# VectorE in GpSimd's place after the last attention head, values ahead of the out block, and final roots for groups of rows

## The chip, the cores and the metric

The kernel runs on one core of a Trainium2 chip. A core has TensorE (PE, matrix products into PSUM banks), VectorE (DVE), ScalarE (ACT), GpSimd (POOL) and SyncE (SP, which here only issues DMAs), each with its own queue of instructions in order. They wait for each other through semaphores. The metric is the device time of one execution in microseconds; less is better.

## What is computed

One layer of a hybrid step: an attention head group and an mLSTM head group side by side, an output projection over both, a SwiGLU feed-forward part, and a last RMS norm. There are 128 context tokens and 1024 latent tokens, so nine rows of 128 tokens (row 0 is context), and a width of 1024. Cut to what the change touches:

```python
mix = jnp.concatenate([attn_o, hm], axis=-1) @ w_out
x = x + g1 * mix
h2 = rmsnorm(x, norm2_w) * (1 + sc2) + sh2
g, u = jnp.split(h2 @ w_gu, 2, axis=-1)
x = x + g2 * ((jax.nn.silu(g) * u) @ w_down)
y = x * lax.rsqrt(jnp.mean(x * x, axis=-1, keepdims=True) + EPS) * final_norm_w
```

Products are made more exact by splitting operands into a high and a low part, so that a product is three matmuls: high by high, high by low, low by high.

## The kernel before, in words

**Attention.** `step(n)` is called for the 64 pairs of a row and a head, and then for some more n until all tasks are done. Its order is written out by hand: products of scores, then `fl.run("PE")`, then the value products of a finished pair of heads (`value_products`, L1054: 18 matmuls of the transposed weights phT and plT with the values into `po`), then the softmax of this head. `fl` is a filler: tasks such as the output projection of a row (`mix_task`) yield the engine that they need next and a cost, and `fl.run` resumes those that fit.

**Output projection and second norm.** `value_sums` scales the value products on ACT (L1059, L1060, `ol`) and adds two halves on POOL into `oT` (L1062). When a row's four pairs are in, `mix_copies` casts `oT` to a high part on ACT (L1420) and subtracts it on POOL for the low part (L136, `kst`, by L1421). `out_block` (L1143 to L1145) makes 12 matmuls into a bank, for each half of the width. `add_gated` multiplies by the gate on DVE (L1134) and adds to the row on POOL (L1137). Then comes the norm: squares on ACT (L1426, `jk`), a root of small instructions on DVE (L1190 to L1197, `r`), the scaled row on ACT (L1433, `y`), transposes on PE (L115), scale and shift half on ACT (L1452) and half on DVE (L1454, `fl`), and the split into high and low parts `h`: casts on ACT (L1462), subtractions on POOL (L136, by L1463). Two out blocks are made for a row. The last row, 8, has no attention step behind it.

**Feed-forward part.** It begins behind row 8's out blocks and the transposes of row 7's norm; row 8's norm is made within it. Its first gate products (L1181 to L1183) use rows whose `h` has long been ready. Weights are loaded (`braw`, `wdt`), measured, scaled and split (`wpair`, L1606 on ACT and L1607 on DVE). DVE and POOL add slices of `h` up (`sk`, L1724 on DVE, L1726 on POOL). From here on a list scheduler sets the order within each engine's queue. The PSUM pool gives out eight banks; `bank()` takes the next.

**End.** After the last group's gates, the final loop goes over the nine rows. For each half of a row, PE makes 12 down products (L1834 to L1836) into a bank; DVE scales by the gate (L1136) and adds to the row (L1137); ACT sums the squares (L1921). After a row's first half POOL multiplies it by the norm's gain `fw` (L1924). After the second half DVE makes the root (L1923, then the twelve instructions of `rsqrt`, L126 to L132, ten of them each waiting for the one before). ACT scales the first half (L1927) and DVE the second, with `fw` in the same instruction (L1928). Each half leaves as a DMA of 256 KB (L1929 from ACT's queue, L1930 from SP's).

Of the kernel before, what the change touches and what calls it, by code (L numbers as in the profile page):

```python
# [8 lines left out]
F32 = mybir.dt.float32  # L9
# [10 lines left out]
P = 128  # L20
# [26 lines left out]
def hybrid_step(ctx: ExitStack, tc: tile.TileContext, I: dict, O: dict):  # L47
# [1009 lines left out]
    def value_sums(b, j, po):  # L1057
# [3 lines left out]
        for g in range(2):  # L1061
            pool.tensor_tensor(out=oT[b][64 * g : 64 * g + 64, j, :], in0=ol[:, 1, g * P : (g + 1) * P],  # L1062
                               in1=ol[:, 0, g * P : (g + 1) * P], op=ALU.add)
# [204 lines left out]

    fl = Filler(PE=3.5, ACT=1.9, DVE=2.0)
# [116 lines left out]
    def mix_task(b):  # L1386
        yield "ACT", 0.5, 1, 0, lambda: b in done and (b == 0 and "pools" in at or since(("atO", b - 1, 1)))
        mix_copies(b)
        for n in range(2):
# [4 lines left out]
            add_gated(x1[b], ps, gx[n] if b == 0 else gs[n], n, pool)  # L1394
# [23 lines left out]
    def mix_copies(b):  # L1418
        th, tl = mix
        nc.scalar.copy(th, oT[b])  # L1420
        sub(tl, oT[b], th.bitcast(F32), "pool")  # L1421
# [35 lines left out]
    def norm_split(b, both):  # L1457
        c, i = divmod(b, CB)
        for half in range(2):
# [3 lines left out]
            sub(ol, full, oh, "pool")  # L1463
# [27 lines left out]
    def step(n):  # L1491
# [5 lines left out]
        fl.run("PE")  # L1497
# [3 lines left out]
        elif n % 2 == 1 and (n - 3) // 2 in pairs:  # L1501
            m = (n - 3) // 2
            two = pairs.pop(m)
            now = [value_products(heads[2 * m][0], m % 4, NB, m % 4 // 2, lambda t, i: two[t][:, :, i, :])]
        if n < len(heads):
# [154 lines left out]
    psum["mm"] = ctx.enter_context(tc.tile_pool(name="p8", bufs=8, space=PSUM, reuse_waits="tile"))  # L1660
    pieces[1].load()
# [250 lines left out]
    for b in range(NB):  # L1912
        st = fp.tile([P, 4], F32, name=nm("st"), tag="fst", bufs=4)
        for n in range(2):
            ps = bank()
            for j in range(0, g["nf"], 2):
                down_products(ps, g, j, b, ws[n][j // 2])
            add_gated(x1[b], ps, gate2(b, n), n, inv=g["inv"])
            v = x1[b][:, n * 512 : (n + 1) * 512]
            jk = ft.tile([P, D], BF16, name=nm("jk"), tag="t2", bufs=3)  # L1920
            act(jk[:, 0:512], v, AF.Square, accum_out=st[:, n : n + 1])  # L1921
            if n == 0:
                dve.tensor_scalar(out=st[:, 2:3], in0=st[:, 0:1], scalar1=1.0 / D, scalar2=EPS, op0=ALU.mult, op1=ALU.add)  # L1923
                pool.tensor_tensor(out=v, in0=v, in1=fw[:, 0:512], op=ALU.mult)  # L1924
        r = rsqrt(fp, st[:, 1:2], 1, 1.0 / D, CB, st[:, 2:3])
        lo, hi = x1[b][:, 0:512], x1[b][:, 512:1024]
        act(lo, lo, AF.Copy, scale=r)  # L1927
        dve.scalar_tensor_tensor(out=hi, in0=hi, scalar=r, in1=fw[:, 512:1024], op0=ALU.mult, op1=ALU.mult)  # L1928
        nc.scalar.dma_start(yrow(b)[:, 0:512], lo)  # L1929
        dma(yrow(b)[:, 512:1024], hi)  # L1930
# [52 lines left out]
```

## Time and profile before

| | |
|---|---|
| median of 3 runs | 1612.08 us (1606.82 to 1614.46) |
| the profiled execution's own time | 1611.04 us |
| its span | 1609.3 us |
| mean granted clock of PE | 0.954 |
| PE busy | 1456.1 us, 90% of the span |
| DVE busy | 1141.5 us, 71% |
| ACT busy | 790.6 us, 49% |
| POOL busy | 265.9 us, 17% |

Times in the profile are microseconds from the start of the span. A row of an engine's timeline gives start, length, engine, line and operation, and in brackets the idle time ahead of it with the instruction that ended it. The stages are: input projections and the mLSTM part until about 440, attention heads until about 812, the output projection and norm of the last row until about 866, the feed-forward part until 1590.9 (PE's last product), and the last roots and stores until 1609.3.

### The profile page before, as it was taken

The page shows a single profiled execution, that of the slowest core. Times are in us where ns is not written, and L with a number is a line of the kernel's source. Part 1 is how long each engine was busy: PE and PEld are TensorE (multiplying, and loading weights), DVE is VectorE, ACT ScalarE, POOL GpSimd, SP SyncE. Part 2 cuts the span into 40 slices and gives each one's busy share as a digit, 9 for nine tenths or more (in the row PEclk, how much of TensorE's full clock was granted, in tenths as well). Part 3 has the DMA queues.
Part 4 walks back from the last instruction along what each step waited for, and adds up shares of the span by engine and source line. Part 5 has one row for each costly group of instructions (what it writes and reads, how often), then busy time and mean ns, then how long its engine had stood idle before and what let it go on. Part 6 is the DMA issues. An engine that isn't in the chain of part 4 may idle for free. (4 is left out here: it accounts for less than half of the span.)

```text
span 1609.3 us, 23125 instructions
## 1 busy us (share of the span) xinstructions
PE 1456.1 (90%) x8417; PEld 900.6 (56%) x8417; DVE 1141.5 (71%) x2572; ACT 790.6 (49%) x1504; POOL 265.9 (17%) x284
## 2 busy tenths in 40 slices
PE   5899999899596799987769999999999999999995
PEld 2655666576354577765545556546545645656542
DVE  3944355848866687876758898777767867787478
ACT  3744343435465666777756535425504523654123
POOL 0411021403216522333344000000000000000001
PEclk8899999999788899998879999999999999999998
DMA  9445452301175689656544323432433332322303
GB/s 350 128 134 154 104 142 66 72 6 19 34 174 108 119 188 204 130 96 122 89 121 135 115 92 118 131 92 93 133 115 99 112 120 90 118 92 81 104 1 118
DMA packets 281687, 181.83 MB, mean 113 GB/s; under 512 B 167302, under 2 KB 253782, under 8 KB 281574
## 3 DMA queue, kind: packets, MB, share of 16 engines
q1 hardware_dynamic: 280150, 177.96, 42.3%
q10 hardware_dynamic: 1424, 2.40, 0.4%
q8 instruction: 66, 1.08, 0.3%
q14 instruction: 47, 0.39, 0.1%
HBM read 122.71 MB, written 19.29 MB: 88 GB/s over the span
## 5 line engine op out<-in xcount | busy, mean ns | idle before, releaser
L1606 ACT ACTIVATE wpair<-braw,fv 128x1024 f16<-128x1024 f32 x84 | 93.7, 1139 | 171.7 <-PE mm L1836 94.9
L1835 PE MATMUL mm<-wd,hl 128*128 128x512 f16 x396 | 149.8, 379 | 0.0
L1834 PE MATMUL mm<-wd,hl 128*128 128x512 f16 x396 | 149.6, 379 | 0.0
L1836 PE MATMUL mm<-wd,hl 128*128 128x512 f16 x396 | 142.3, 379 | 0.0
L1111 PE MATMUL S<-kst,qT 128*128 128x512 f32 (+1 forms) x384 | 98.4, 397 | 47.2 <-ACT pr L1119 45.4
L1181 PE MATMUL mm<-h,wpair 128*128 128x384 f16 x416 | 137.3, 330 | 4.3 <-DVE r L1190 3.2
L1183 PE MATMUL mm<-h,wpair 128*128 128x384 f16 x416 | 136.8, 330 | 2.4 <-DVE wpair L1607 2.4
L1182 PE MATMUL mm<-h,wpair 128*128 128x384 f16 x416 | 137.2, 330 | 0.0
L1607 DVE SCALAR_TENSOR_TENSOR wpair<-braw,fv,wpair 128x1024 f16<-128x1024 f32 x84 | 106.5, 1281 | 37.4 <-ACT wpair L1606 37.4
L1924 POOL TENSOR_TENSOR x<-x,fw 128x512 f32<-128x512 f32 x9 | 11.7, 1304 | 710.8 <-ACT jk L1921 710.8
L500 PE MATMUL wi<-ipair,hT 128*128 128x384 f16 (+2 forms) x384 | 124.4, 325 | 2.8 <-ACT ipair L217 2.8
L501 PE MATMUL wi<-ipair,hT 128*128 128x384 f16 (+2 forms) x384 | 124.5, 324 | 0.0
L502 PE MATMUL wi<-ipair,hT 128*128 128x384 f16 (+2 forms) x384 | 123.9, 323 | 0.0
L1115 DVE TENSOR_REDUCE st<-S 128x1 f32<-128x1152 f32 x64 | 86.7, 1355 | 44.8 <-PE S L1111 44.2
L1518 DVE SCALAR_TENSOR_TENSOR pl<-pr,st,ph 128x1152 f16<-128x1152 f32 x64 | 94.3, 1474 | 28.2 <-ACT ph L1510 25.6
L1510 ACT ACTIVATE ph<-pr,st 128x1152 f16<-128x1152 f32 x64 | 80.3, 1254 | 68.8 <-issue 59.7
L1111 PEld LDWEIGHTS S<-kst,qT 128*128 128x128 f32 x384 | 70.9, 210 | 71.7 <-ACT pr L1119 57.8
L1119 ACT ACTIVATE pr<-S,st 128x1152 f32<-128x1152 f32 x64 | 78.0, 1219 | 28.3 <-DVE st L1115 27.7
L1136 DVE SCALAR_TENSOR_TENSOR t<-mm,gm,gl 128x512 f32<-128x512 f32 x96 | 70.6, 744 | 29.0 <-PE mm L1836 28.8
L1137 DVE TENSOR_TENSOR x<-x,t 128x512 f32<-128x512 f32 x108 | 78.1, 736 | 1.3
L1737 PE MATMUL mm<-h,wpair 128*128 128x384 f16 x240 | 78.2, 326 | 0.0
L1736 PE MATMUL mm<-h,wpair 128*128 128x384 f16 x240 | 78.2, 326 | 0.0
(462 smaller groups left out, 3625.7 us busy)
## 6 DMA issues: line engine op xcount, KB each, us to landing
wd<-wd_d SPq DMA_DIRECT2D x58, 512.0 KB
braw<-in_w_gu_dram SPq DMA_DIRECT2D x44, 512.0 KB
a4s<-in_w_ada_dram SPq DMA_DIRECT2D x32, 512.0 KB
wdt<-in_w_down_dram SPq DMA_DIRECT2D x22, 512.0 KB
wd_d<-wdt SPq DMA_DIRECT2D x22, 512.0 KB
aw<-in_w_ada_dram SPq DMA_DIRECT2D x16, 512.0 KB
x<-in_x_sample_dram SPq DMA_DIRECT2D x16, 512.0 KB
iraw<-in_w_in_dram SPq DMA_DIRECT2D x32, 256.0 KB
```

What stands on the lines that cost most here:

```text
L500: mm(ps[:, :n], ah, wh[:, k % 2, c0 : c0 + n], start=(k == 0), stop=False)
L501: mm(ps[:, :n], ah, wl[:, k % 2, c0 : c0 + n], start=False, stop=False)
L502: mm(ps[:, :n], al, wh[:, k % 2, c0 : c0 + n], start=False, stop=(k == KD - 1))
L1111: mm(S[:, lo:hi], qTs[b][:, h, :], kst[kv][:, t, lo:hi], start=(t == 0), stop=(t == 1))
L1181: mm(ps, wh[:, k, :], th[:, k, :], start=(k == 0), stop=False)
L1182: mm(ps, wh[:, k, :], tl[:, k, :], start=False, stop=False)
L1183: mm(ps, wl[:, k, :], th[:, k, :], start=False, stop=(k == KD - 1))
L1518: dve.scalar_tensor_tensor(out=pl, in0=pr, scalar=st[:, 3:4], in1=ph, op0=ALU.mult, op1=ALU.subtract)
L1607: dve.scalar_tensor_tensor(out=t[:, 1], in0=raw, scalar=sc, in1=t[:, 0], op0=ALU.mult, op1=ALU.subtract)
L1834: mm(ps, ah, w[:, k, 0], start=(j + k == 0), stop=False)
L1835: mm(ps, ah, w[:, k, 1], start=False, stop=False)
L1836: mm(ps, al, w[:, k, 0], start=False, stop=(j + k == g["nf"] - 1))
```

## The change

There are four parts.

First, `side()` names the engine for additions and subtractions in the tasks: DVE from the first step without a head (n of 64 and more), POOL before. It is used in `value_sums`, in the second instruction of `add_gated` in `mix_task`, in `mix_copies` and in the norm's split.

Second, in steps with n of 64 and more the value products and their sums stand ahead of `fl.run("PE")`.

Third, ahead of the feed-forward part `bank()` is called twice, and the two tiles are not used.

Fourth, the final loop goes over groups of rows (0, 1, 2), (3, 4, 5), (6, 7) and (8). A group has one root for all of its rows (L1938 adds the two sums of squares, then `rsqrt` over 3, 2 or 1 columns). POOL multiplies both halves of a row by `fw` (L1937) except the last half of row 8. ACT scales whole rows (L1943), and a whole row leaves as one DMA of 512 KB, in turn from ACT's and SP's queue (L1944). Row 8 is finished as before (L1947, L1948).

```diff
@@ value_sums
-            pool.tensor_tensor(out=oT[b][64 * g : 64 * g + 64, j, :], in0=ol[:, 1, g * P : (g + 1) * P],
+            side().tensor_tensor(out=oT[b][64 * g : 64 * g + 64, j, :], in0=ol[:, 1, g * P : (g + 1) * P],
...
+    def side():
+        return dve if fl.step >= len(heads) else pool
...
@@ mix_task
-            add_gated(x1[b], ps, gx[n] if b == 0 else gs[n], n, pool)
+            add_gated(x1[b], ps, gx[n] if b == 0 else gs[n], n, side())
@@ mix_copies
-        sub(tl, oT[b], th.bitcast(F32), "pool")
+        sub(tl, oT[b], th.bitcast(F32), "pool" if side() is pool else "dve")
@@ norm_split
-            sub(ol, full, oh, "pool")
+            sub(ol, full, oh, "pool" if side() is pool else "dve")
@@ step(n)
-        fl.run("PE")
+        if n < len(heads):
+            fl.run("PE")
...
+        if n >= len(heads):
+            for v in late + now:
+                value_sums(*v)
+            late[:], now = [], []
+            fl.run("PE")
...
     psum["mm"] = ctx.enter_context(tc.tile_pool(name="p8", bufs=8, space=PSUM, reuse_waits="tile"))
+    for _ in range(2):
+        bank()
...
-    for b in range(NB):
-        st = fp.tile([P, 4], F32, name=nm("st"), tag="fst", bufs=4)
...
-            act(jk[:, 0:512], v, AF.Square, accum_out=st[:, n : n + 1])
-            if n == 0:
-                dve.tensor_scalar(out=st[:, 2:3], in0=st[:, 0:1], scalar1=1.0 / D, scalar2=EPS, op0=ALU.mult, op1=ALU.add)
-                pool.tensor_tensor(out=v, in0=v, in1=fw[:, 0:512], op=ALU.mult)
-        r = rsqrt(fp, st[:, 1:2], 1, 1.0 / D, CB, st[:, 2:3])
...
+    for rows in ((0, 1, 2), (3, 4, 5), (6, 7), (8,)):
+        st = fp.tile([P, 2, CB], F32, name=nm("st"), tag="fst", bufs=2)
+        ss = fp.tile([P, CB], F32, name=nm("ss"), tag="fss", bufs=2)
+        k = len(rows)
...
+                act(jk[:, 0:512], v, AF.Square, accum_out=st[:, n, i : i + 1])
+                if n == 0 or k > 1:
+                    pool.tensor_tensor(out=v, in0=v, in1=fw[:, n * 512 : (n + 1) * 512], op=ALU.mult)
+        dve.tensor_tensor(out=ss[:, 0:k], in0=st[:, 0, 0:k], in1=st[:, 1, 0:k], op=ALU.add)
+        r = rsqrt(fp, ss[:, 0:k], k, 1.0 / D, CB)
+        for i, b in enumerate(rows):
+            ri = r[:, i : i + 1]
+            if k > 1:
+                act(x1[b], x1[b], AF.Copy, scale=ri)
+                (dma if i % 2 else nc.scalar.dma_start)(yrow(b), x1[b])
+                continue
...
```

The rows below are the instructions as each built program holds them for an engine, in order; a bracket names the engines and queues that a row waits for.

TensorE behind the transposes for row 6's norm, before: the end of row 7's second out block (`mm_8132`), and then the last pair of value products, which is row 8's (`phT_8024`, `plT_8025`). Row 8's two out blocks follow these.

```order
L1144 MATMUL mm_8132<-whi_6782,kst_4270 128x512
L1145 MATMUL mm_8132<-whi_6781,kst_4271 128x512
L1054 LDWEIGHTS vs [waits DMAHW6_49,DMAHW4_49]
L1054 MATMUL po_4797<-phT_8024,vs 128x256 [waits Activation_49]
L1054 LDWEIGHTS vs [waits DMAHW7_49]
L1054 MATMUL po_4797<-plT_8025,vs 128x256 [waits DMAHW5_49]
```

The same place in the changed kernel: the pair stands right behind the transposes (L115).

```order
L115 MATMUL mm_8114<-ident,y_8093 128x128 [waits DVE_49]
L115 MATMUL mm_8114<-ident,y_8093 128x128 x3
L1054 LDWEIGHTS vs [waits DMAHW6_49,DMAHW4_49]
L1054 MATMUL po_4797<-phT_8024,vs 128x256 [waits Activation_49]
L1054 LDWEIGHTS vs [waits DMAHW7_49]
L1054 MATMUL po_4797<-plT_8025,vs 128x256 [waits DMAHW5_49]
```

Row 7's out block (12 matmuls, now `mm_8155`) follows behind the pair's 18, and then row 8's two.

POOL's queue in the same stretch, before: sums of values, subtractions, additions to the row, and then the first sums `sk`.

```order
L1062 TENSOR_TENSOR oT_7859<-ol_8114 64x128 x2
L136 TENSOR_TENSOR h_1418_7626<-fl_8095,h_1418_7626 128x4x128 x2
L136 TENSOR_TENSOR h_1508_8163<-fl_8123,h_1508_8163 128x4x128 x2
L1137 TENSOR_TENSOR x_2_5702<-x_2_5702,t_1509_8168 128x512
L1062 TENSOR_TENSOR oT_7859<-ol_8171 64x128 x2
L136 TENSOR_TENSOR kst_4271<-oT_7859,kst_4270 128x512
L1726 TENSOR_TENSOR sk_8337<-h_1334_7140,h_1418_7626 128x384
L1726 TENSOR_TENSOR sk_8337<-sk_8337,h_1334_7140 128x384
L1726 TENSOR_TENSOR sk_8337<-sk_8337,h_1418_7626 128x384
L1137 TENSOR_TENSOR x_2_5702<-x_2_5702,t_1514_8204 128x512
```

POOL in the changed kernel, from the same add to row 7 on:

```order
L1137 TENSOR_TENSOR x_2_5702<-x_2_5702,t_1495_8052 128x512 [waits DVE_49,Pool_49]
L1737 TENSOR_TENSOR sk_8339<-h_1334_7140,h_1418_7626 128x384 [waits DMAHW3_49,DMAHW2_49,DMAHW4_49,DMAHW1_49,DMAHW5_49,DMAHW0_49,DMAHW7_49,PE_49,Activation_49]
L1737 TENSOR_TENSOR sk_8339<-sk_8339,h_1334_7140 128x384 [waits Pool_49]
L1737 TENSOR_TENSOR sk_8339<-sk_8339,h_1418_7626 128x384 [waits DVE_49,Pool_49]
L1737 TENSOR_TENSOR sk_8410<-h_1334_7140,h_1418_7626 128x384 [waits DMAHW2_49,DMAHW5_49,DVE_49,Activation_49]
L1737 TENSOR_TENSOR sk_8410<-sk_8410,h_1334_7140 128x384 [waits Pool_49]
L1737 TENSOR_TENSOR sk_8410<-sk_8410,h_1418_7626 128x384 [waits Pool_49]
L1737 TENSOR_TENSOR sk_8481<-h_1334_7140,h_1418_7626 128x384
```

The ten instructions ahead of the sums are gone from POOL's queue and stand in DVE's, so that the sums `sk` are next in POOL's.

In the third part, the first gate tile of the built program lies in PSUM bank 0 in both kernels, and in both it waits for the last `fl` of row 7's norm on DVE (L1454 before, L1457 in the changed kernel).

DVE in the final loop, before, where row 0's root chain is under way between the half rows' L1136 and L1137:

```order
L1136 SCALAR_TENSOR_TENSOR t_2568_15054<-mm_15041,gm_14791,gl_8573 128x512 [waits PE_49]
L130 TENSOR_TENSOR rt_14943<-ry_14942 128x1 [waits DVE_49]
L128 TENSOR_SCALAR ry_15001<-rh_15003 128x1 [waits DVE_49]
L1923 TENSOR_SCALAR st_15020<-st_15020 128x1 [waits Activation_49]
L1137 TENSOR_TENSOR x_0_4863<-x_0_4863,t_2568_15054 128x512 [waits DVE_49]
L131 SCALAR_TENSOR_TENSOR rt_14943<-rt_14943,rv_14941 128x1 [waits DVE_49]
L130 TENSOR_TENSOR rt_15002<-ry_15001 128x1 [waits DVE_49]
L1136 SCALAR_TENSOR_TENSOR t_2576_15093<-mm_15080,gm_14791,gl_8571 128x512 [waits PE_49]
```

DVE in the changed kernel, behind row 2, the last of the first group:

```order
L1137 TENSOR_TENSOR x_0_4863<-x_0_4863,t_2561_15014 128x512 [waits DVE_49]
L1136 SCALAR_TENSOR_TENSOR t_2570_15058<-mm_15045,gm_14793,gl_8573 128x512 [waits PE_49,Activation_49]
L1938 TENSOR_TENSOR ss_14905<-st_14904 128x3 [waits Activation_49]
L1137 TENSOR_TENSOR x_1_5701<-x_1_5701,t_2570_15058 128x512 [waits DVE_49]
L126 TENSOR_SCALAR rv_15021<-ss_14905 128x3 [waits DVE_49]
L1136 SCALAR_TENSOR_TENSOR t_2573_15077<-mm_15064,gm_14793,gl_8575 128x512 [waits PE_49]
L127 TENSOR_SCALAR rh_15024<-rv_15021 128x3 [waits DVE_49]
```

Up to row 2's last half no root instruction stands in DVE's queue any more; L1938 waits for ACT's squares with the next half row's L1137 queued behind it.

More of the change, by code (lines that the diff above doesn't have):

```diff
@@ L1911, in hybrid_step @@
     ws = [[down_piece(g, j, n, ("whi", "wlo")[n]) for j in range(0, g["nf"], 2)] for n in range(2)]
-    for b in range(NB):
-        st = fp.tile([P, 4], F32, name=nm("st"), tag="fst", bufs=4)
[L1914 to L1921, printed above, removed]
-            if n == 0:
-                dve.tensor_scalar(out=st[:, 2:3], in0=st[:, 0:1], scalar1=1.0 / D, scalar2=EPS, op0=ALU.mult, op1=ALU.add)
-                pool.tensor_tensor(out=v, in0=v, in1=fw[:, 0:512], op=ALU.mult)
-        r = rsqrt(fp, st[:, 1:2], 1, 1.0 / D, CB, st[:, 2:3])
[L1926 to L1930, printed above, removed]
+    for rows in ((0, 1, 2), (3, 4, 5), (6, 7), (8,)):
[3 more added lines that the diff above has]
+        for i, b in enumerate(rows):
+            for n in range(2):
+                ps = bank()
+                for j in range(0, g["nf"], 2):
+                    down_products(ps, g, j, b, ws[n][j // 2])
+                add_gated(x1[b], ps, gate2(b, n), n, inv=g["inv"])
+                v = x1[b][:, n * 512 : (n + 1) * 512]
+                jk = ft.tile([P, D], BF16, name=nm("jk"), tag="t2", bufs=3)
+                act(jk[:, 0:512], v, AF.Square, accum_out=st[:, n, i : i + 1])
[3 more added lines that the diff above has]
+        r = rsqrt(fp, ss[:, 0:k], k, 1.0 / D, CB)
+        for i, b in enumerate(rows):
+            ri = r[:, i : i + 1]
[3 more added lines that the diff above has]
+                continue
+            lo, hi = x1[b][:, 0:512], x1[b][:, 512:1024]
+            act(lo, lo, AF.Copy, scale=ri)
+            dve.scalar_tensor_tensor(out=hi, in0=hi, scalar=ri, in1=fw[:, 512:1024], op0=ALU.mult, op1=ALU.mult)
+            nc.scalar.dma_start(yrow(b)[:, 0:512], lo)
+            dma(yrow(b)[:, 512:1024], hi)
```

## The prediction

> **What bounds the kernel now.** I read the stages first, by engine, to see where TensorE (PE) still loses time; the last column but two is the clock that PE was granted.
>
> ```profile
> core 0: us, PE busy (x) PEld busy (x) DVE busy (x) ACT busy (x) POOL busy (x), PEclk, DMA share, GB/s
> 808.00:866.00 58.00, 41.84 (x214) 27.39 (x213) 36.21 (x89) 35.00 (x69) 25.31 (x24) 0.85 0.38 115
> 866.00:960.00 94.00, 92.29 (x527) 51.74 (x526) 86.19 (x180) 43.30 (x76) 6.71 (x5) 0.99 0.36 111
> 960.00:1240.00 280.00, 279.81 (x1589) 155.12 (x1587) 211.49 (x418) 119.12 (x207) 0.00 (x0) 1.00 0.36 111
> 1240.00:1544.00 304.00, 303.81 (x1736) 169.42 (x1733) 215.09 (x429) 119.32 (x213) 0.00 (x0) 1.00 0.32 100
> 1544.00:1590.90 46.90, 46.86 (x217) 21.05 (x216) 42.86 (x125) 18.98 (x45) 8.86 (x7) 1.00 0.12 46
> 1590.90:1609.30 18.40, 0.00 (x0) 0.00 (x0) 13.71 (x53) 5.56 (x12) 2.88 (x2) 0.63 0.38 143
> ```
>
> From 960 to 1590.9 PE is busy for 630.5 of 630.9 us. So a microsecond that PE gets back between 808 and 866, where it is idle for 16 and cold for part of the rest, moves everything behind it and reaches the end. The second place is the 18.4 us after PE's last product. The change touches these two places only.
>
> Next I read PE's order of time through the transition. The bracket is idle time before the row and what ended it.
>
> ```profile
> 817.57 0.79 PE L1143 MATMUL mm<-wlo,kst 128*128 128x512 f32 x1 [4.76 <-DVE fl L1454]
> ...
> 821.27 0.39 PE L1143 MATMUL mm<-whi,kst 128*128 128x512 f32 x1
> 821.50 0.40 PE L1144 MATMUL mm<-whi,kst 128*128 128x512 f32 x1
> ...
> 821.98 0.28 PE L1054 MATMUL po<-phT,vs 128*128 128x256 f16 x1
> ...
> 828.21 0.79 PE L1145 MATMUL mm<-whi,kst 128*128 128x512 f32 x1 [0.62 <-POOL kst L136]
> ...
> 840.62 0.48 PE L1181 MATMUL mm<-h,wpair 128*128 128x384 f16 x1 [3.16 <-DVE r L1190]
> ...
> 864.44 0.34 PE L1183 MATMUL mm<-h,wpair 128*128 128x384 f16 x1 [2.43 <-DVE wpair L1607]
> ```
>
> After 4.76 us of idleness row 7's out block (12 products, L1143 to L1145) starts cold: it takes 4.4 us, though its last products follow at 0.23. The last pair of value products (L1054, row 8) stands behind that block. What releases row 8's two out blocks (828.21) is a subtraction on GpSimd (POOL), which hangs on that pair through ScalarE (ACT). The first gate products wait until 840.62.
>
> **Values first.** The pair's transposed weights must be there before the block. The transposes are issued on SP; an earlier pair shows how long one takes until PE may use it.
>
> ```profile
> 441.58 1.27 SPq L1098 DMA_TRANSPOSE plT<-pl  x1
> ...
> 444.76 0.37 PE L1054 MATMUL po<-plT,vs 128*128 128x256 f16 x1 [0.63 <-DMA plT<-pl]
> ```
>
> ```profile
> 810.53 1.32 SPq L1519 DMA_TRANSPOSE plT<-pl  x1
> ```
>
> That is 3.2 us, so the pair can run from 810.5 + 3.2 = 813.7. Its 18 products took 821.98 to 824.1, 2.1 us, and end at 815.9, inside the 4.76 us in which PE stood idle: they cost nothing there. On SP, behind the transposes, only one load of down weights changes its place, by one row; no row above waits for it. With PE busy until 815.9 I take the out block as warm: 12 at 0.23 is 2.8 us. The bound: cold as now, 4.4.
>
> The block itself waits for `fl`, the scaled transposes of row 6's norm, which waits for two subtractions `h`. These subtractions are among the work that VectorE (DVE) takes over.
>
> ```profile
> 813.85 2.26 POOL L136 TENSOR_TENSOR h<-fl,h 128x512 f16<-128x512 f32 x2
> ...
> 826.88 1.28 POOL L136 TENSOR_TENSOR kst<-oT,kst 128x512 fp32r<-128x512 f32 x1 [0.73 <-ACT kst L1420]
> ...
> 829.10 2.31 POOL L1726 TENSOR_TENSOR sk<-sk,h 128x384 f32<-128x384 f32 x2
> ...
> 836.05 2.81 POOL L1137 TENSOR_TENSOR x<-x,t 128x512 f32<-128x512 f32 x2 [4.64 <-DVE t L1134]
> ...
> 848.43 0.91 POOL L1726 TENSOR_TENSOR sk<-h,h 128x384 f32<-128x384 f16 x1
> ```
>
> ```profile
> 824.15 0.47 ACT L1059 ACTIVATE ol<-po,vsc 64x256 f32<-64x256 f32 x1 [5.33 <-PE po L1054]
> ```
>
> ```profile
> 828.21 1.23 DVE L1724 TENSOR_TENSOR sk<-h 128x384 f32<-128x384 f16 x1
> ...
> 831.87 0.55 DVE L1724 TENSOR_TENSOR sk<-sk,h 128x384 f32<-128x384 f32 x1
> ...
> 852.86 0.87 DVE L1586 SCALAR_TENSOR_TENSOR fv<-fv 128x1 f32<-128x1 f32 x1
> ...
> 854.23 1.16 DVE L1724 TENSOR_TENSOR sk<-sk,h 128x384 f32<-128x384 f32 x1
> 855.43 1.14 DVE L1724 TENSOR_TENSOR sk<-sk,h 128x384 f32<-128x384 f32 x1
> ```
>
> On POOL a subtraction of 128x512 takes 1.13 to 1.28 us. DVE has no row of that form here; its nearest, the add L1137 below, holds it for 0.60. I take 0.6, with 0.55 and 1.28 as the ends; at 1.28 the five of them on the path would cost 3.4 more and leave almost nothing of the gain below. But POOL does not fall silent. Its sums sk (L1737, L1726 before) no longer have the transition's adds ahead of them in its queue: nine of them run from about 813 on, at 0.9 each, where six ran at 848 and later. And a DVE add with both inputs in SBUF waits while one of them runs: 1.23 beside POOL at 828 to 831, 0.55 without. The Trainium skill says the same in "SBUF — State Buffer", section "Who interferes with whom": such an instruction contends with a GpSimd one that reads SBUF, and the second to issue blocks fully. The rows agree, 1.23 for 0.55. By that rule the gain worked out next is 3.6; without it, 5.6.
>
> So I let the two engines alternate. From 813.2, when the first cast is there, a POOL sum and a subtraction h take turns: 2 x (0.9 + 0.6) ends at 816.2. On POOL both ended at 813.85 + 2.26 = 816.1. So the out block starts at 817.6, as before, and ends warm at 820.4. ACT now scales the pair's values (two of 0.47, at 824.15 before) right behind fl, by 818.6. Then DVE: two small adds 0.9 (0.48 each on POOL), two subtractions h 1.2, L1134 0.65, L1137 0.6, the subtraction kst 0.6, and two POOL sums of 0.9 or a little more in between: 818.6 + 3.95 + 2.0 = about 824.6. Before, kst ended at 828.16. **Gain 3.6**; without a POOL sum 5.6. Row 8's out blocks, row 7's root chain on DVE (three sums beside it before, three now) and y follow with the lead unchanged. The two L1137 of 2.81 us on POOL become 1.2 on DVE ahead of row 7's last fl, but their neighbours no longer collide (2.10 for two before): 0.2 more. First gate products at 840.62 - 3.8 = 836.8.
>
> **Other banks.** In the built program the first gate tile lies in bank 0 in both kernels (the two tiles that are never used take no place), and it still waits for the last fl on DVE, which empties bank 0. So I cost this edit at nothing: the 3.16 us wait stays, and the cold start behind it (13 products at 0.32 in place of 0.163, 2.1 us). If it worked, both would go: up to 5.
>
> **VectorE from 850 to 864.** It never pauses there, and PE waits at 864.44 for its wpair. Four DVE rows lie longer than alone, beside POOL's sums of 848 to 856: 0.13, 0.73, 0.61 and 0.59 us over. The first six of those sums are done by then. **Gain 2.1** (0 to 2.1). PE then waits for nothing new until 960; DVE has 8 us to spare of 94 there.
>
> **The tail.** From 1555 on DVE adds the products of 18 half rows, and it is the last link:
>
> ```profile
> 1555.86 0.69 DVE L1137 TENSOR_TENSOR x<-x,t 128x512 f32<-128x512 f32 x1
> 1556.46 0.74 DVE L1136 SCALAR_TENSOR_TENSOR t<-mm,gm,gx 128x512 f32<-128x512 f32 x1
> ...
> 1557.34 0.15 DVE L1923 TENSOR_SCALAR st<-st 128x1 f32<-128x1 f32 x1
> 1557.41 1.79 DVE L1137 TENSOR_TENSOR x<-x,t 128x512 f32<-128x512 f32 x1
> ```
>
> ```profile
> 1557.38 1.27 POOL L1924 TENSOR_TENSOR x<-x,fw 128x512 f32<-128x512 f32 x1 [680.64 <-ACT jk L1921]
> ```
>
> ```profile
> 1600.78 0.63 ACT L1921 ACTIVATE jk<-x 128x512 bf16<-128x512 f32 x1 [2.30 <-DVE x L1137]
> 1601.32 0.18 ACT L1921 ACTIVATION_READ_ACCUMULATOR jk<-x 128x1 f32 x1
> ...
> 1604.51 0.72 ACT L1927 ACTIVATE x<-x,ry 128x512 f32<-128x512 f32 x1 [1.49 <-DVE ry L132]
> 1605.26 0.35 ACTq L1929 DMA_DIRECT2D out_y_sample_dram<-x  x1
> ```
>
> ```profile
> L1928 DVE SCALAR_TENSOR_TENSOR x<-x,ry,fw 128x512 f32<-128x512 f32 x7 | 5.2, 744 | 0.0
> L130 DVE TENSOR_TENSOR rt<-ry 128x1 f32<-128x1 f32 x24 | 4.6, 195 | 0.0
> ```
>
> ```profile
> 1606.00:1607.40 1.40, 0.00 (x0) 0.00 (x0) 0.00 (x0) 0.00 (x0) 0.00 (x0) 0.50 0.97 361
> ```
>
> DVE's last L1137 ends at about 1600.75, ten microseconds after PE. Removed before that point: seven L1928 at 0.66 (4.6 us) and 65 of 117 small root instructions, some 0.07 from start to start (4.5). Added: eight multiplies on POOL, each of which can block an L1137 by 1.79 - 0.69 = 1.1 us, and three waits of L1938 for ACT's sum of squares (0.8 behind L1137: 0.63 and 0.18). ACT is held by three scalings of whole rows in a run; a half row takes 0.72, so a whole one takes 0.72 to 1.44, I take 1.1. The floor is PE's end and one pair: 1590.9 + 1.4 = 1592.3. If every POOL block bites: 1555.1 + 18 x 1.26 + 17 x 1.1 + 39 x 0.07 + 3 x 1.9 = 1604.9. While DVE has a backlog the blocks bite; once it has caught up (1.26 of POOL and 0.6 make 1.87 a half row, PE needs 2.59) they fall into PE's pace. I take the middle, 1598.4.
>
> Behind it: 0.85 for the squares, 2.4 for the root's twelve links (L130's mean, 0.195), 0.72 to scale: issue at +4.0, as before (4.5). But rows 6 and 7 are scaled only now, and 1.57 MB leaves in place of the last 0.5: at 361 GB/s 4.4 us from +2.7, then 1.85 as now from the last byte to the end of the span: +8.9 to +9.7, I take 9.3 (8.55 now). End 1607.7 for 1609.3: **gain 1.6**, between -4.9 and +7.7.
>
> **Sum.** 3.8 + 2.1 + 1.6 = 7.5 off the profiled execution's 1611.04: 1603.5. That execution is 1.0 below the median of the runs, 1612.08, so the median goes to **1604.6**.
>
> **Rivals.**
> First, the engines do not collide in the transition, and the gate start turns out warm: 5.6 + 0.2 + 2.1, up to 5 from the banks, 1.6: gain 10 to 14, 1598 to 1602. For it: the collision is read off other instructions than the moved ones. Against: the gate tile's bank and its wait are unchanged.
> Second, that the change does not do what it says: the banks part, counted at nothing above, is that case; it is in the forecast.
> Third, the POOL multiplies take DVE's place as the bound of the tail. If every block bites the tail loses 4.9, and 1 us is left of the gain: 1611. If ACT's three scalings in a row (3.3 us, twice) also delay the multiplies and the next root's wait, DVE ends at 1604.9 + 6.6 = 1611.5, the tail loses 11.5, and the kernel is slower than before by 5.6: 1617.7. It decides from 1605.9 on, where the loss passes the 5.9 us of the transition. For it: two of the nine blocks are visible rows of 1.79. Against: PE's pace of 2.59.
> Fourth, the lead at 836.8 is lost to DVE between 866 and 960, where it is busy for 86 of 94 us: then 1.6 is left, 1610.5.
>
> **How the numbers follow.** Forecast (gain 4 to 9.5) 0.52, first rival 0.20, third 0.20 (0.08 of it slower than before), fourth 0.08. A measurement here tells about 0.5%, 8 us, from no change: that is 1604.0. The first rival and somewhat under half of the forecast lie below it: faster 0.43; slower by as much only the far end of the third: 0.07; the same 0.50. The range leaves out 1 in 10 at each end: 1597 to 1611.5.
>
> **What would show it.** Value products ahead of the out block, at 813.7; kst on DVE ending near 824.6; first gate product near 837 and still cold behind a wait for DVE; PE's last product 5.9 earlier; the last L1137 7.5 behind PE's end (9.9 before). Wrong it would be if PE's end moves by less than 3 or more than 9, or if DVE's last add follows PE's end by more than 12.

## The result, and the profile after

The changed kernel takes 1600.74 us, the median of ten runs (1596.80 to 1604.54). The kernel before, run beside it on the same chips, takes 1609.31 us (ten runs, 1605.96 to 1614.46). The ratio is 0.9948 with a 95% interval of 0.9932 to 0.9964: 8.6 us less, where 7.5 were forecast. (The forecast of 1604.6 counted from 1612.08, the median of the three runs known then. Of its 3.9 us above 1600.74, 2.8 come from that starting point and 1.1 from the gain.) The profiled execution took 1598.72 us with a span of 1596.9 and a mean clock of 0.959.

Two spans cannot simply be subtracted here. The first view is VectorE's timeline at the end of attention: the last row maximum (L1115), in the kernel before and in the changed one.

```profile
801.80 1.35 DVE L1115 TENSOR_REDUCE st<-S 128x1 f32<-128x1152 f32 x1
```

```profile
797.87 1.35 DVE L1115 TENSOR_REDUCE st<-S 128x1 f32<-128x1152 f32 x1
```

Up to this instruction both programs hold the same instructions in the same order, yet it starts 3.9 us earlier in this execution of the changed kernel. In the eleven kernels below it starts anywhere from 797.7 to 802.5, whatever they change; the reason was not looked for. So 3.9 of the 12.4 us between the two spans is not the change. Below, times count from this instruction: **G** is the start of the first gate product, **E** the end of PE's last product, and **tail** the time from there to the end of the span. PE's last product, before and after:

```profile
1590.48 0.38 PE L1836 MATMUL mm<-wd,hl 128*128 128x512 f16 x1
```

```profile
1580.66 0.38 PE L1847 MATMUL mm<-wd,hl 128*128 128x512 f16 x1
```

Before, G is 38.82, E 789.06 and the tail 18.44; after, 34.52, 783.17 and 15.86. The change brings 4.30 by G, 1.59 more by E and 2.58 in the tail, 8.47 together. That agrees with the 8.57 between the medians.

The stages of the changed kernel, with the columns of the view by stretches shown before:

```profile
808.00:860.00 52.00, 41.24 (x217) 26.09 (x216) 44.46 (x108) 32.16 (x63) 10.80 (x9) 0.90 0.46 142
860.00:960.00 100.00, 96.81 (x563) 54.69 (x561) 89.23 (x181) 47.56 (x86) 6.71 (x5) 1.00 0.34 103
...
1544.00:1581.04 37.04, 37.04 (x172) 16.60 (x170) 33.41 (x58) 16.61 (x36) 20.57 (x14) 1.00 0.16 62
1581.04:1596.90 15.86, 0.00 (x1) 0.00 (x0) 9.80 (x31) 5.04 (x11) 3.75 (x3) 0.61 0.40 156
```

The transition is shorter, and PE's clock in it went from 0.85 to 0.90. But PE idles 3.2 us between 860 and 960, where it idled 1.7 between 866 and 960 before. POOL is busy for 20.6 of the last 37 us of the products.

PE's timeline through the transition of the changed kernel follows. PE is called warm at a granted clock near 1.00 and cold near 0.50 (PEclk, the third column from the end above).

```profile
809.88 0.28 PE L1054 MATMUL po<-plT,vs 128*128 128x256 f16 x1 [0.86 <-DMA plT<-pl]
...
813.60 0.50 PE L1143 MATMUL mm<-wlo,kst 128*128 128x512 f32 x1 [1.69 <-DVE fl L1457]
...
820.01 0.79 PE L1145 MATMUL mm<-whi,kst 128*128 128x512 f32 x1 [2.14 <-DVE kst L136]
...
832.39 0.48 PE L1181 MATMUL mm<-h,wpair 128*128 128x384 f16 x1 [1.46 <-DVE fl L1457]
...
854.65 0.34 PE L1183 MATMUL mm<-h,wpair 128*128 128x384 f16 x1 [0.60 <-DVE wpair L1616]
...
886.53 0.39 PE L1591 MATMUL mm<-fv,ones 128*128 128x2 f32 x2 [1.48 <-ACT jk L1586]
```

The value products of row 8 stand ahead of the out block, which waits 1.69 us in place of 4.76 and starts warm (0.50 in place of 0.79 for its first product). It starts 15.7 behind the row maximum, before and after: what it waits for has not become earlier. The gain appears at the next row: row 8's last operand `kst` is there at 820.01, 22.14 behind the maximum, where it was 26.41. The wait at 854.65 has shrunk from 2.43 to 0.60, and 886.53 is a wait that was not there before.

VectorE's timeline in the transition, and then POOL's:

```profile
815.29 2.02 DVE L136 TENSOR_TENSOR h<-fl,h 128x512 f16<-128x512 f32 x2
817.23 0.68 DVE L1134 TENSOR_TENSOR t<-mm,gl 128x512 f32<-128x512 f32 x1
817.94 0.69 DVE L1137 TENSOR_TENSOR x<-x,t 128x512 f32<-128x512 f32 x1
818.56 1.40 DVE L136 TENSOR_TENSOR kst<-oT,kst 128x512 fp32r<-128x512 f32 x1
819.88 1.27 DVE L1735 TENSOR_TENSOR sk<-h 128x384 f32<-128x384 f16 x1
...
823.57 0.56 DVE L1735 TENSOR_TENSOR sk<-sk,h 128x384 f32<-128x384 f32 x1
```

```profile
815.39 1.36 POOL L1737 TENSOR_TENSOR sk<-h,h 128x384 f32<-128x384 f16 x1 [2.56 <-DVE oT L1062]
816.84 2.57 POOL L1737 TENSOR_TENSOR sk<-sk,h 128x384 f32<-128x384 f32 x2
819.37 1.36 POOL L1737 TENSOR_TENSOR sk<-h,h 128x384 f32<-128x384 f16 x1
```

The two engines take turns, as the prediction assumed: a sum of POOL's that takes 0.91 alone takes 1.36, and DVE's `kst` and first `sk` last 1.40 and 1.27 beside POOL. Run 5 below shows the same two without a POOL sum beside them: 0.68 and 0.55.

VectorE, POOL and ScalarE in the tail of the changed kernel, a fence each. PE's last product ends at 1581.04.

```profile
1580.04 0.69 DVE L1137 TENSOR_TENSOR x<-x,t 128x512 f32<-128x512 f32 x1
1581.87 0.71 DVE L1938 TENSOR_TENSOR ss<-st 128x2 f32<-128x2 f32 x1 [1.13 <-ACT jk L1935]
1582.61 1.19 DVE L126 TENSOR_SCALAR rv<-ss 128x2 f32<-128x2 f32 x1
...
1585.49 0.16 DVE L131 SCALAR_TENSOR_TENSOR rt<-rt,rv 128x2 f32<-128x2 f32 x1
...
1586.08 1.22 DVE L131 SCALAR_TENSOR_TENSOR rt<-rt,rv 128x2 f32<-128x2 f32 x1
...
1587.99 0.69 DVE L1137 TENSOR_TENSOR x<-x,t 128x512 f32<-128x512 f32 x1
```

```profile
1581.30 2.48 POOL L1937 TENSOR_TENSOR x<-x,fw 128x512 f32<-128x512 f32 x2 [2.50 <-ACT jk L1935]
1586.02 1.26 POOL L1937 TENSOR_TENSOR x<-x,fw 128x512 f32<-128x512 f32 x1 [2.24 <-ACT jk L1935]
```

```profile
1579.48 1.13 ACT L1943 ACTIVATE x<-x,ry 128x1024 f32<-128x1024 f32 x1
1580.52 0.61 ACT L1935 ACTIVATE jk<-x 128x512 bf16<-128x512 f32 x1
```

DVE's last add (L1137) ends 7.64 behind PE, 9.89 before. Between PE's end and this add stands the root of rows 6 and 7. Two of its small instructions last 1.19 and 1.22 while POOL multiplies; the same L131 takes 0.16 alone. Ahead of the root DVE idles 1.13 for ACT's squares, and the last row of ACT's three whole-row scalings stands ahead of those.

### The profile page after: what moved, and what is told of

Its sections match the earlier page's. It is cut to its first block, busy times and chain, and to the rows that moved or that the text cites. A ratio compares the mean times of both kernels' runs of the same rounds, so it can differ in the third digit from the quotient of the medians.

```text
span 1596.9 us, 23049 instructions
## 1 busy us (share of the span) xinstructions
PE 1453.4 (91%) x8417; PEld 898.0 (56%) x8417; DVE 1143.6 (72%) x2513; ACT 793.9 (50%) x1504; POOL 264.9 (17%) x278
## 5 line engine op out<-in xcount | busy, mean ns | idle before, releaser
L1937 POOL TENSOR_TENSOR x<-x,fw 128x512 f32<-128x512 f32 x17 | 24.3, 1450 | 696.0 <-ACT jk L1935 696.0
L1115 DVE TENSOR_REDUCE st<-S 128x1 f32<-128x1152 f32 x64 | 86.7, 1355 | 44.7 <-PE S L1111 44.1
L1136 DVE SCALAR_TENSOR_TENSOR t<-mm,gm,gl 128x512 f32<-128x512 f32 x96 | 70.5, 743 | 29.0 <-PE mm L1847 28.9
L1137 DVE TENSOR_TENSOR x<-x,t 128x512 f32<-128x512 f32 x111 | 77.6, 711 | 1.6
```

## The experiments

The kernels in one view; before and after are the profiled executions. Medians of the kernel before were 1608.98 us beside the first four, 1609.44 beside the next four and 1608.66 beside the last three.

| kernel | G | E | tail | median us | ratio and 95% interval |
|---|---|---|---|---|---|
| before | 38.82 | 789.06 | 18.44 | | |
| the change | 34.52 | 783.17 | 15.86 | 1600.74 | 0.9948 (0.9932 to 0.9964) |
| 1 VectorE only | 39.33 | 787.47 | 17.86 | 1606.78 | 0.9989 (0.9978 to 1.0001) |
| 2 values first only | 35.39 | 785.56 | 17.85 | 1605.75 | 0.9978 (0.9968 to 0.9988) |
| 3 both | 34.54 | 784.90 | 18.12 | 1601.44 | 0.9957 (0.9941 to 0.9973) |
| 4 tail only | 38.69 | 789.29 | 15.92 | 1607.13 | 0.9992 (0.9981 to 1.0002) |
| 5 a third of the sums `sk` | 33.88 | 781.34 | 15.90 | 1597.97 | 0.9923 (0.9905 to 0.9942) |
| 6 banks taken | 32.93 | 782.17 | 15.92 | 1599.48 | 0.9937 (0.9921 to 0.9953) |
| 7 groups, multiplies on VectorE | 34.45 | 783.23 | 12.01 | 1596.64 | 0.9918 (0.9893 to 0.9942) |
| 8 no late multiplies | 34.75 | 782.80 | 12.78 | 1601.29 | 0.9945 (0.9925 to 0.9966) |
| 9 a root for each row, multiplies on POOL | 34.66 | 783.19 | 17.78 | 1602.42 | 0.9968 (0.9955 to 0.9981) |
| 10 is 6 and 7 | 32.80 | 782.17 | 11.97 | 1594.53 | 0.9920 (0.9906 to 0.9933) |
| 11 is 10 without POOL for rows 6 to 8 | 34.01 | 783.10 | 11.85 | 1594.86 | 0.9916 (0.9902 to 0.9930) |

G, E and tail are each read from one execution, but several kernels hold the same program in a stretch, and their rows show how well a figure repeats. With the change's transition (runs 3, 7, 8 and 9 besides the change) G is 34.45 to 34.75 and E 782.80 to 783.23, but for 784.90 in run 3. With the final loop of before (runs 1 to 3) the tail is 17.85 to 18.44, with that of the change (runs 4 to 6) 15.86 to 15.92. So the tail's gain of 2.58 is 2.0 to 2.6.

### The parts alone

**1. VectorE only.** `side()` and its four uses as in the change; the order of the steps, the banks and the tail as before. Against the kernel before:

```diff
+    def side():
+        return dve if fl.step >= len(heads) else pool
...
-            add_gated(x1[b], ps, gx[n] if b == 0 else gs[n], n, pool)
+            add_gated(x1[b], ps, gx[n] if b == 0 else gs[n], n, side())
...
```

> Only the first part: DVE takes the adds and subtractions, the order of the steps, the banks and the final loop are those of before. Three intervals are read from each trace: from the start of the last row maximum (L1115) to the first gate product (38.8 us before, 34.5 with the whole change), from there to PE's last product (L1115 to its end: 789.1 before, 783.2 with the change), and from PE's last product to the end of the span (18.4 before, 15.9). My theory: the value pair still stands behind the cold out block, so the first gate product comes at 37.5 to 38.8, at most 1.3 earlier; but POOL's sums are early, DVE is free of them from 850 on, and PE's last product comes 2.1 earlier, at 787.0 (gain 2 to 3.4 in all). Rival, that the faster engine alone makes the gain: 34.5 and 783.2.

G came out half a microsecond later than before, so that expectation missed; E was 1.6 earlier, where 2.1 was expected. The out block still waits 4.80 us for `fl` (4.76 before), with the pair behind it. Row 8's out block then resumes 0.8 earlier against the row maximum (25.60 behind it, 26.41 before), but DVE's next work, its sums and row 7's root, now has six of POOL's sums beside it where it had three. The transposes behind that root come 0.8 later than before. PE's row for them, before and in run 1:

```profile
836.19 1.27 PE L115 MATMUL mm<-ident,y 128*128 128x128 f32 x8 [1.28 <-ACT y L1433]
```

```profile
837.65 0.66 PE L115 MATMUL mm<-ident,y 128*128 128x128 f32 x4 [2.63 <-ACT y L1436]
```

What DVE alone gives, it gives behind G: POOL's sums are done earlier, PE's wait for `wpair` around 860 falls from 2.43 to 0.60, and PE goes on 1.6 us sooner against the row maximum.

**2. Values first only.** Banks and final loop are those of before. Against the change:

```diff
     def side():
-        return dve if fl.step >= len(heads) else pool
+        return pool
```

> Only the second part: in steps without a head the value products and sums stand ahead of the filler's PE work; POOL keeps its adds and subtractions. My theory: the out block runs warm behind the pair (2.8 us for 4.4), ACT scales row 8's values some 6 us earlier, but POOL then has two small sums, two subtractions, an L1137 and the subtraction kst in a row (0.97 + 2.28 + 1.26 + 1.28 = 5.8 us) from about 818.6: kst done at 824.5 to 825.5 on the clock of before, a gain of 2.7 to 3.7 at the first gate product (35.1 to 36.1 us behind the last L1115), and the sums stay late, so that PE's last product keeps this gain and no more (785.4 to 786.4). Rival, that the order is worth nothing without DVE: 38.8 and 789.1.

G 35.39 and E 785.56, both as expected: 3.4 us of the 4.3 at G come from the order alone, with POOL subtracting as before.

**3. Both,** with the tail of before and without the two calls of `bank()`. Against the change:

```diff
-    for _ in range(2):
-        bank()
...
-    for rows in ((0, 1, 2), (3, 4, 5), (6, 7), (8,)):
+    for b in range(NB):
```

> First and second part together, banks and final loop as before. My theory: the whole gain of the transition, 34.5 us to the first gate product and 783.2 to PE's last product, as in the whole change, and the end 18.4 us behind it as before: a gain of 5.9 in all, a ratio of 0.9963. Rival, that the unused banks matter: the first gate product later than in the whole change by 1.5 or more.

G is that of the change, 34.54. The parts alone give 3.5 and 1.6 at E, 5.1 of the 5.89: together they are worth 0.8 more. With the pair ahead of the out block DVE brings G from 35.39 (run 2) to 34.54; alone it brought nothing there. E itself came out 1.7 later than in the change, by a cold run of PE whose rows stand further below.

**4. Tail only.**

> Only the fourth part, the final loop in groups; all else as before. My theory: PE's last product as before (789.1), the end 15.9 us behind it for 18.4, a gain of 2.6 in all, a ratio of 0.9984. Rival, that POOL's added multiplies hold DVE up where the stretch starts from the old state of the queues: 18.4 us or more.

Against the kernel before:

```diff
-    for b in range(NB):
+    for rows in ((0, 1, 2), (3, 4, 5), (6, 7), (8,)):
```

The tail is 15.92, that of the change, and E stays where it was. By the medians this alone can't be told from no change (the interval holds the 2.5 us of the trace as well as nothing); the tails tell it, 15.92 against 17.85 to 18.44.

### The transition

**The banks.** Built without the two calls of `bank()`, the changed kernel is the same program: the same instructions with the same waits on all five engines. To see what the edit was to do, a write makes the two banks really taken.

**6. Banks taken.**

```diff
     for _ in range(2):
-        bank()
+        dve.memset(bank()[0:1, 0:1], 0.0)
```

> The whole change, and DVE writes one element into each of the two tiles, so that they take a bank (in the change itself the two tiles take none). In the built program the first gate product then waits for no fl any more. My theory: it follows the transposes directly, 1.5 us earlier, at 33.0 behind the last L1115, still cold, since PE idles 1.5 and 0.9 us just before; behind it DVE has only 0.9 us of slack before its full stretch, so PE's last product gains 0.9, 782.3 for 783.2. Rival, that the bank is worth what the wait and the cold run come to, 3.6: 779.6. Other rival, that the lead is lost altogether behind it: 783.2.

PE's timeline at the first gate product of this kernel, and its waits from 830 to 960 (what waits for what: us in total, times, longest):

```profile
831.74 0.52 PE L1181 MATMUL mm<-h,wpair 128*128 128x384 f16 x1
```

```profile
PE mm L1591 <- ACT jk L1586: 3.2, 2, 1.7
PE mm L1181 <- ACT wpair L1615: 2.6, 2, 2.1
```

G and E are as expected. The wait for `fl` ahead of the first gate product is gone (1.46 in the change), and G is 1.6 earlier. The products still start cold, at 0.52. Of the 1.6 us, 1.0 reaches PE's end: the next waits for ACT's `wpair` are 2.6 us, 1.1 in the change. The forecast's "up to 5" for working banks was far too much.

**5. A third of the sums `sk`.** Of three additions for a slice only the first is made; two terms are left out of the sums.

```diff
-            for out, in0, in1, op in ((s3, ah[:, k], bh[:, k], ALU.subtract), (s3, s3, al[:, k], ALU.add), (s3, s3, bl[:, k], ALU.subtract)):
+            for out, in0, in1, op in ((s3, ah[:, k], bh[:, k], ALU.subtract),):
```

> The whole change, but each of POOL's four triples of sums sk is one instruction (the two that add the low parts are left out), so that 3 instead of 9 of them run in the transition. It measures what POOL's sums cost DVE there. My theory: the pair of subtractions h waits once instead of twice (0.9 less), behind the out block one sum stands in DVE's way for two and more (0.9 to 1.8 less), and the root chain loses another 1.2: first gate product 31 to 33 us behind the last L1115 (34.5 with the change), PE's last product 780 to 782 (783.2), a ratio of 0.993 to 0.9935 to before. Rival, that the sums only fill gaps: 34.5 and 783.2.

E is as expected (781.34), G is not: 33.88 where 31 to 33 was expected. VectorE and PE in this kernel:

```profile
817.62 0.68 DVE L136 TENSOR_TENSOR kst<-oT,kst 128x512 fp32r<-128x512 f32 x1
818.22 0.55 DVE L1735 TENSOR_TENSOR sk<-h 128x384 f32<-128x384 f16 x1
...
825.94 0.56 DVE L136 TENSOR_TENSOR sums<-sk,sums 128x384 f16<-128x384 f32 x1 [1.88 <-ACT sums L1739]
826.41 0.21 DVE L1197 TENSOR_SCALAR r<-r 128x1 f32<-128x1 f32 x1
```

```profile
818.36 0.50 PE L1145 MATMUL mm<-whi,kst 128*128 128x512 f32 x1 [1.41 <-DVE kst L136]
```

Row 8's out block resumes 1.4 us earlier against the row maximum: 0.7 because row 7's out block began 0.7 earlier (15.0 behind the maximum), and 0.7 because `kst`, with no POOL sum beside it, takes 0.68 in place of 1.40. More than half of that is lost again: DVE reaches a `sums` subtraction early and waits 1.88 us for ACT's cast, with the last step of row 7's root (L1197) queued behind it. So these collisions cost 1.4 at `kst`, but only 0.6 at G. The expected E came by another way: at the wait for `wpair` PE is only 0.3 ahead of the change, and the rest is the wait of 1.48 for `jk`, at 886.53 in the change, which this kernel does not have.

### The tail

In the changed tail, POOL multiplies both halves of a row. The theory was that this relieves DVE and that most of what is left are fixed chains; the rival, that POOL's multiplies block DVE for more than they relieve.

**7. Groups, with VectorE's multiplies.** Row groups as in the change, but the second half gets `fw` on DVE with the scaling, as before the change.

```diff
-                if n == 0 or k > 1:
-                    pool.tensor_tensor(out=v, in0=v, in1=fw[:, n * 512 : (n + 1) * 512], op=ALU.mult)
+                if n == 0:
+                    pool.tensor_tensor(out=v, in0=v, in1=fw[:, 0:512], op=ALU.mult)
...
-            if k > 1:
-                act(x1[b], x1[b], AF.Copy, scale=ri)
-                (dma if i % 2 else nc.scalar.dma_start)(yrow(b), x1[b])
-                continue
```

> The whole change, but in the final loop the second halves of the rows are multiplied by DVE behind the root, as before, and leave as two DMAs of 256 KB; only the grouping of the roots is kept. My theory, that the gain of the tail comes from the multiplies taken from DVE (8 x 0.66) as much as from the fewer root instructions: the end 17 to 18 us behind PE's last product (15.9 with the change, 18.4 before). Rival, that POOL's multiplies cost DVE as much as they save, so that grouping is all of the gain: 15.5 or less.

The tail is 12.01 where the theory had 17 to 18: it fell, and the rival held. The groups of instructions on VectorE in the last stretch, from 1540 (the change) and 1544 (this kernel) on, first of the changed kernel, then of this one (busy us, mean ns, then idle time ahead and what ended it):

```profile
L1137 DVE TENSOR_TENSOR x<-x,t 128x512 f32<-128x512 f32 x18 | 15.3, 849 | 0.3
...
L1938 DVE TENSOR_TENSOR ss<-st 128x3 f32<-128x3 f32 (+2 forms) x4 | 1.9, 473 | 2.8 <-ACT jk L1935 2.8
```

```profile
L1137 DVE TENSOR_TENSOR x<-x,t 128x512 f32<-128x512 f32 x18 | 13.0, 721 | 0.3
...
L1938 DVE TENSOR_TENSOR ss<-st 128x3 f32<-128x3 f32 (+2 forms) x4 | 1.2, 295 | 1.3 <-ACT jk L1935 1.2
```

DVE has nine L1944 where it had one L1948, 5 to 6 us more to do at 0.7 each, and its last add still ends 4.7 us earlier, 2.91 behind PE. The adds are 0.13 shorter each, the waits for ACT's squares 1.6 less in all, and most of the blocked root instructions are gone. The root of rows 6 and 7 (L1938) starts 1.55 ahead of PE's end, where the change starts it 0.83 behind, and from there to the last add are 4.5 us in place of 6.8. ACT scales half rows here (0.7 each) where the change scales whole ones (1.13) ahead of the squares; how much of the earlier start is ACT's and how much is the blocks', no run separates. Here rows 6 to 8 are stored together: the end is 9.1 behind DVE's last add.

**8. No late multiplies.** POOL's multiplies by `fw` for rows 6 and 7 and for the first half of row 8 are left out.

```diff
-                if n == 0 or k > 1:
+                if b < 6:
```

> The whole change, without POOL's multiplies by the gain for rows 6, 7 and 8 (five instructions; these rows leave unmultiplied, except the last half). It measures what the late multiplies cost DVE by the shared access to SBUF. In the trace of the change four small or large DVE instructions behind PE's last product stand 0.6, 1.05, 1.1 and 0.5 us longer than alone beside POOL. My theory: these go, the end comes 13 to 13.5 us behind PE's last product (15.9). Rival, that ACT's squares set the pace and DVE's blocked instructions only wait in their shadow: 15.5 or more.

The tail falls to 12.78, a little more than expected; DVE's last add ends 4.55 behind PE. The last five multiplies alone hold 3.1 us. The ratio, 0.9925 to 0.9966, is too wide to show it.

**9. A root for each row, with POOL's multiplies.**

```diff
-    for rows in ((0, 1, 2), (3, 4, 5), (6, 7), (8,)):
+    for rows in ((0,), (1,), (2,), (3,), (4,), (5,), (6,), (7,), (8,)):
...
-                if n == 0 or k > 1:
+                if n == 0 or b < 8:
...
-            if k > 1:
+            if b < 8:
...
-                (dma if i % 2 else nc.scalar.dma_start)(yrow(b), x1[b])
+                (dma if b % 2 else nc.scalar.dma_start)(yrow(b), x1[b])
```

> The whole change, but with a root for each row, as before; POOL multiplies both halves (rows 0 to 7) and rows leave as one DMA of 512 KB. With before (a root for each row, DVE multiplies second halves: the end 18.4 us behind PE's last product), the whole change (grouped roots, POOL: 15.9) and e7 (grouped, DVE: 12.0) it fills the table of the two edits in the final loop. My theory by now: POOL's eight added multiplies cost 3.9 us net and grouping saves 6.4, and the two add up: 21 to 23.5 us. Rival, that with many root instructions POOL's multiplies come in the place of DVE's and cost nothing: 17.5 to 19.

The tail is 17.78: the theory in which the two edits' costs add up (21 to 23.5) fell, and the rival's 17.5 to 19 held. With it the square is complete, tails in us:

| | second halves times `fw` on VectorE | on POOL |
|---|---|---|
| a root for each row | 17.9 to 18.4 (before, runs 1 to 3) | 17.8 (run 9) |
| a root for a group | 12.0 (run 7) | 15.9 (the change) |

The upper row is not the multiplies alone: run 9 also stores whole rows and adds the two sums of squares in the instruction L1938. With a root for each row, taking eight multiplies off DVE gives nothing clear of the spread. DVE's last add ends where it did, 9.89 behind PE before and 9.94 in run 9:

```profile
1600.06 0.69 DVE L1137 TENSOR_TENSOR x<-x,t 128x512 f32<-128x512 f32 x1
```

```profile
1591.58 0.68 DVE L1137 TENSOR_TENSOR x<-x,t 128x512 f32<-128x512 f32 x1
```

What the blocks of the added multiplies reach there are root instructions: L131 lasts 358 ns in the mean of its 27 in run 9, 152 before. With grouped roots DVE comes into PE's pace, and moving the multiplies costs 3.9, by blocks and by ACT's longer scalings together. Grouping is worth 5.8 to 6.4 by itself; the change, with both edits, is 2.0 to 2.6 below before.

### What the runs point to

**10. Banks taken, and the multiplies on VectorE** (the edits of 6 and 7).

> The whole change with e6 (banks that are really taken) and e7 (second halves multiplied by DVE) together. My theory: the gains add up, PE's last product 782.2 behind the last L1115 and the end 12.0 behind that; 13.3 us less than before, a ratio of 0.9917 (e7 alone 12.3, e6 alone 9.4 by the same intervals of the traces). Rival, that they meet on DVE: 0.9924 or more.

G, E and tail are those of 6 and 7, so the two add up: 1594.53 us, 0.9920 of the kernel before (0.9906 to 0.9933), where 0.9917 was expected. The kernel before is slower well beyond the interval. By the ratios run 10 is 4.5 us under the change (0.0028 of 1609), but the two intervals just touch (0.9932 and 0.9933), so that this rests on the traces: E 782.17 and a tail of 11.97, for 783.17 and 15.86. From 7 and 11 it can't be told apart.

**11. As 10, and no POOL for rows 6 to 8.**

```diff
-                    pool.tensor_tensor(out=v, in0=v, in1=fw[:, 0:512], op=ALU.mult)
+                    (dve if b > 5 else pool).tensor_tensor(out=v, in0=v, in1=fw[:, 0:512], op=ALU.mult)
```

> As e10, and for rows 6, 7 and 8 DVE multiplies the first halves too (three instructions of 0.6), so that no POOL instruction stands beside DVE's last ones. My theory: in e7 POOL's two late multiplies lengthen one root instruction by 1.05 and another by 0.5, and L1136 behind them comes late; three times 0.6 take their place, two of them ahead of PE's last product: the end 11.3 to 12 us behind PE's last product. Rival, that DVE's added work stands on the path: 12.5 or more.

The tail is 11.85, 0.1 less than in 10, and the ratio is the same. DVE's last add is 2.68 behind PE and 9.2 ahead of the end: what is left is one row's chain and the stores. (G and E are about 1 us later in this execution: the out block began 16.7 behind the row maximum, 15.7 in run 10. In the 5 us from 804.4 on, ahead of that block, PE's clock was 0.50 here and 0.71 in the same stretch of run 10.)

## Why the prediction was right

**Values first** went as worked out. From the transposes' issue to PE's use are 3.3 us (3.2 forecast), the pair hides in the idle time, and the block starts warm at the same distance from the row maximum. Run 2 shows that this part carries 3.4 of the 4.3 us at G.

**kst, gain 3.6.** Measured 4.27. The chain started where it was put (the small adds 16.8 behind the maximum; the forecast's 818.6 is the same 16.8), and took 5.3 us in place of 6.0. The two terms that were too large are the small adds (0.6 for the pair, not 0.9) and POOL's sums, put at 2.0: in the rows, the pair of `h` lasts 2.02 (twice the 0.68 of a `kst` alone is 1.36) and `kst` 1.40, 1.4 over together. Run 5, with `kst` at 0.68, shows the part at `kst`. The **0.2** at the two L1137 didn't show: G moved by 4.30 where 3.8 was forecast.

**850 to 864, gain 2.1.** The step is there: PE's wait for `wpair` fell by 1.83, and run 1 shows the same fall with DVE's part alone. But PE had lost 0.28 of its lead on the way: from G to the first wait for ACT's `wpair` are 19.67 us, 19.39 before. PE's clock in the second 4 us behind G was 0.91, where it was 0.98 before; the cold start lasted longer in this execution. At E 1.59 was left. That 4.30 + 1.59 gives 5.89, the forecast's 5.9, is in part luck: one term was 0.5 too small and the other 0.5 too large.

**"PE then waits for nothing new until 960"** was wrong, at no cost. The 4 us behind the wait at `wpair`, before and after, in the view by stretches:

```profile
864.40:868.40 4.00, 3.96 (x15) 2.01 (x16) 4.00 (x9) 1.90 (x5) 0.00 (x0) 0.61 0.96 265
```

```profile
854.60:858.60 4.00, 3.95 (x25) 2.40 (x26) 4.00 (x9) 1.90 (x5) 0.00 (x0) 1.00 0.92 248
```

Before, the wait of 2.43 was followed by a cold run (clock 0.61, 15 products); after, PE stays warm (25 products) and is ten products, 1.6 us, further ahead, a gain that the forecast had not counted. It went into the new wait of 1.48 at 886.53, where PE needs ACT's squares `jk`. Behind 886 PE's lead is what it was at 854.65, 5.86 against the row maximum.

**The banks, 0.** Right: the program is the same without them. The mechanism named, an unused tile takes no place, is confirmed by run 6, in which a write makes it take one.

**The tail, 1.6.** Measured 2.58, 2.0 to 2.6 by the repeats. DVE's last add was put at 7.5 behind PE and came at 7.64. (The middle of the forecast's two bounds, 1592.3 and 1604.9, is 1598.6, not the 1598.4 that it took.) The term that failed is "+8.9 to +9.7, I take 9.3" for the time behind it: it was 8.22. The changed kernel's last stores in the view by stretches:

```profile
1591.30:1595.50 4.20, 0.00 (x0) 0.00 (x0) 1.34 (x5) 0.99 (x2) 0.00 (x0) 0.50 0.97 375
1595.50:1596.90 1.40, 0.00 (x0) 0.00 (x0) 0.00 (x0) 0.00 (x0) 0.00 (x0) 0.50 0.00 0
```

The 1.57 MB start 2.6 behind the add, as forecast (2.7), and take 4.2 us (4.4). From the last byte to the end are 1.4 where 1.85 was taken over from before, and the squares' and root's chain for row 8 alone, 4.2 us to the issue, hides behind the stores of rows 6 and 7.

**The rivals.** The first (no collisions, warm gate start) is excluded: `kst` shows 1.40, the gate starts cold at 0.48. The second is the banks. The third, that POOL's multiplies become the bound of the tail, did not show in the result, but its mechanism was at work: 3.9 us of what grouping gives, 5.8 to 6.4, went there, and ACT's three scalings in a row delayed the squares, as it said. The forecast put DVE's end midway between PE's pace and every block biting, and that it came out there is luck. At DVE's last add grouping alone gives 7.0 (run 7) and the moved multiplies take 4.7 of it back. The forecast counted the seven L1928 taken from DVE as a relief of 4.6; run 9 has that relief and its last add does not move. The fourth did not come: DVE is busy for 89 of the 100 us from 860 on, and the lead at 960 is whole.

## What to carry to other kernels

Work that is moved off an engine is not a gain by itself. Count what it blocks from its new place, and at which instruction, since a chain of tiny instructions pays the whole length of the block. In the final loop the same move gave nothing that could be told with a root for each row, and cost 3.9 us once the roots were grouped. Give each edit of a bundle its own run, best in a square of both with and without: here one edit undid more than half of another, and the sum looked like a success. Where something is only allocated, look in the built program whether it takes its place.

## What the hardware showed that was not expected

**The same wait, cold or not.** PE in the changed kernel and in run 3, which hold the same instructions here; timeline and then stretches of 4 us:

```profile
945.76 0.38 PE L1591 MATMUL mm<-fv,ones 128*128 128x2 f32 x2 [1.70 <-ACT jk L1586]
```

```profile
945.70:949.70 4.00, 3.94 (x25) 2.49 (x26) 3.85 (x13) 2.68 (x6) 0.00 (x0) 1.00 0.00 0
```

```profile
946.30 0.38 PE L1591 MATMUL mm<-fv,ones 128*128 128x2 f32 x2 [1.71 <-ACT jk L1586]
```

```profile
946.30:950.30 4.00, 4.00 (x15) 2.08 (x16) 2.92 (x10) 2.62 (x5) 0.00 (x0) 0.57 0.00 0
```

After a wait of 1.70 the clock stays at 1.00 in one execution; after 1.71 it falls to 0.57 in the other, with 15 products in 4 us in place of 25. In the 4 us up to the end of the wait PE was busy for 2.4 in the first and 2.3 in the second. The same wait, 1.70 or 1.71, stands in all thirteen traces, and in the other eleven the clock stays at 1.00. The cold run cost the 1.7 us by which run 3's E is late. So the row before a wait does not tell whether what follows is cold, and an E of one execution can be off by this much. The Trainium skill, "TensorE: Matmul & The Clock Gate", section "Part 1: The HAM clock gate (the “warmup” mystery)", says that the window in which activity is watched runs freely, so that the point of transition varies from run to run. The two rows fit that; it also speaks of about 3.4 us of idleness before the clock is lowered, and here 1.71 were enough once.

**Blocks reach tiny instructions.** A root instruction of 128x2 (L126, L131), 0.15 to 0.16 alone, lasted 1.19 to 1.22 in the changed kernel's tail, beside POOL multiplies of 1.26. The trace of before has such a row too, L130 at 1598.08 with 1.22, but the forecast counted blocks for the large adds only.
